# Three of four feed-forward blocks open with plain row blocks, their scratch is placed elsewhere, and the planner starts them with engines already busy

## The chip, the cores and the metric

The kernel runs on one core of a Trainium2 chip. The metric is the device time of one launch in microseconds (us); lower is better. An engine's name is as the profile has it: PE is the matmul engine, PEld its weight loads, DVE, ACT and POOL are the three elementwise engines, SP issues most of the DMAs.

## The reference, cut to what matters

A hybrid encoder of two layers works on 512 + 32 tokens of width 1024. Each layer has two SwiGLU feed-forward blocks at half step, so there are four feed-forward blocks in the program, and they alone are touched by the change. Between them lie a Mamba-2 mixer (first layer), an attention with shared keys and values (second layer), and a gated input at the end of each layer.

```python
def swiglu(h, w_gate, w_up, w_down):
    return (jax.nn.silu(h @ w_gate) * (h @ w_up)) @ w_down

x = x + 0.5 * swiglu(rms_norm(x, ffn_norm[i, 0]), ffn_w_gate[i, 0], ffn_w_up[i, 0], ffn_w_down[i, 0])
...
x = x + 0.5 * swiglu(rms_norm(x, ffn_norm[i, 1]), ffn_w_gate[i, 1], ffn_w_up[i, 1], ffn_w_down[i, 1])
```

## The kernel before, in words

All 544 tokens (T) stand side by side in the free dimension, in two halves of 272 (H); the 1024 model rows are 8 chunks of 128 (KC). Every float32 product is made of three matmuls: weight and input are each split into a high and a low part (`whi`/`wlo`, `xh`/`xl`, `hh`/`hl`), and high*high, high*low and low*high are added in PSUM. Splitting a 128x1024 weight is a copy (ACT or POOL) that gives `whi`, and a subtraction (mostly DVE) that gives `wlo`.

A feed-forward block (class `Sevens`, lines 532 to 893) has 22 row blocks of 128 hidden rows. A hidden row block needs a gate and an up product. There are two forms:

- the plain form (unit "p", called the old form in the change's title): for one row block and one of gate/up, 8 chunks x 3 matmuls x 2 halves = 48 matmuls of 128x272. The method `plain` (line 824) then multiplies both products by the norm's factor `r` out of PSUM into two scratch tiles `g` and `u`, applies silu, multiplies, and splits the result into `hh` and `hl` (`hidden`).
- the form by sevens (unit "s"): two row blocks at once by a Strassen-Winograd scheme, seven products in place of eight. Each of the seven steps (`STEPS`, line 530) is 4 chunks x 2 x 3 = 24 matmuls of 128x272. It needs sums of weight quarters (`s`, `a`; DVE or POOL), sums of input quarters (`xf`, class `Forms`, made once per feed-forward block by ACT and DVE), and four scratch tiles `c0` to `c3`, into which ACT copies intermediate products out of PSUM (`save`, line 775: steps 0, 1, 2 and 4 go to `c0`, `c3`, `c1`, `c2`).

`FIRST` (line 49) lists the row blocks of the opening group of each feed-forward block; a pair in parentheses goes by sevens. `GROUPS` lists the other groups, all pairs. After each group its part of the down product follows, interleaved with the next group's steps. The four PSUM banks have the roles A, B, D, X; plain blocks use (A, B) and (D, X) in turn.

The order of instructions on PE, DVE, ACT and POOL in a feed-forward block is set by a planner (class `Plan`, line 61) while the program is built: every piece of work is a generator that asks for slots of a resource ("get"), events ("wait") or engine time, and the planner repeatedly emits the request that can start earliest by its own cost table. `plan.busy` is the time until which it takes an engine as occupied when the block starts: zero for all, and 3.0 for PE in the first block (which has an opening by hand, `opening`, line 428). The planner also picks ACT or POOL for a copy and DVE or POOL for a sum by the load it has booked. `raw` is a resource of two buffers (`wraw`) through which all plain and down weights come from memory; weight quarters for the form by sevens have buffers of their own (`a11` to `a22`).

The norm of a block is worked out beside its first products: PE sums the squares with a matrix of minus ones (tile `nones`, right operand names `hh`/`hl`), ACT and DVE make `r` from the result. Blocks one, two and four do so; block three takes `r` ready from the norm before.

Of the kernel before, what the change touches and what calls it, by code (L numbers as in the profile page):

```python
# [4 lines left out]
F32 = mybir.dt.float32  # L5
# [5 lines left out]
P = 128  # L11
# [4 lines left out]
T = TP + TS  # L16
# [29 lines left out]

RGNORM, RSCAN, RCONV, RGATE, ROUT, RSTEP = 39, 4, 20, 45, 2, 41

FIRST = [0, 1, 2, 3], [0, 1, (2, 3)], [0, 1, (2, 3)], [0, 1, (2, 3)]
GROUPS = [(4, 5), (6, 7)], [(8, 9), (10, 11)], [(12, 13), (14, 15)], [(16, 17), (18, 19), (20, 21)]  # L50
AFTER, UNTIL = 3, 14

NH = 6
# [117 lines left out]
def s_cost(n, psum=False):  # L171
    return n / 1200.0 + (0.052 if psum else 0.094)


def v_cost(n):
    return n / 960.0 + 0.069


def _body(tc, io):
# [17 lines left out]
    V, S, G, TE = (Engine(n, e) for n, e in (("V", nc.vector), ("S", nc.scalar), ("G", nc.gpsimd), ("T", nc.tensor)))  # L197
# [4 lines left out]
    with ExitStack() as ctx:  # L202
        const = ctx.enter_context(tc.tile_pool(name="const", bufs=1))
        pool = ctx.enter_context(tc.tile_pool(name="pool", bufs=1))

        def halves(ap):
            return ap.rearrange("p (a b) -> p a b", a=2)
# [324 lines left out]
        class Sevens:  # L532
# [7 lines left out]
            def __init__(self, plan, i, norm, bank, tmp, ring, roles, after, first=(), opened=None, ahead=None, done=None):  # L540
                self.plan, self.i, self.bank, self.tmp, self.ring = plan, i, bank, tmp, ring
                self.groups, self.after, self.opened, self.norm, self.ahead, self.done = (FIRST[i],) + GROUPS, after, opened, norm, ahead, done
                self.roles, self.first = list(roles), first
# [279 lines left out]

            def plain(self, f, pg, pu, banks):
                yield "wait", "r"
                places = ("c2", "c3") if f % 2 else ("sq", "sq")
                for t in places:
                    yield "get", t
                g, u = (self.tmp.tile([P, T], F32, tag=t, name=t) if f % 2 else pool.tile([P, T], F32, tag=t, name=t, bufs=2) for t in places)
                rv = halves(self.norm.r[:, :])  # L830
                yield "W", v_cost(T), lambda: V.tensor_tensor(out=halves(g[:, :]), in0=pg[:, :, :H], in1=rv, op=ALU.mult)
                yield "put", f"b{banks[0]}"
                yield "S", s_cost(T), lambda: S.activation(g, g, AF.Silu), "silu"
                yield "W", v_cost(T), lambda: V.tensor_tensor(out=halves(u[:, :]), in0=pu[:, :, :H], in1=rv, op=ALU.mult)
                yield "put", f"b{banks[1]}"
                yield from self.hidden(f, g, u)
                for t in places:
                    yield "put", t
# [38 lines left out]
            def run(self):  # L877
                plan, (A, B, D, X) = self.plan, self.roles
                self.plain_banks = (A, B), (D, X)
                if self.opened:  # L880
                    plan.busy["T"] = 3.0
                    plan.add(-1, self.first_block((A, B)))
                plan.add(0, self.scale(X))
                plan.add(20, self.dense())
                plan.add(10, self.weights())
                plan.add(9, self.fetch_plain())
                for name in ("a11", "a21", "a22", "a12"):
                    plan.add(9, self.fetch_quarter(name))
                plan.add(5, self.sums())
                ordered.update("TVSG")  # L890
                plan.run()
                ordered.clear()
                return [self.loaded[len(self.units) - 1]] if self.ahead is not None else ()

        def sevens(i, norm, after, bank, tmp, ring, roles, **kw):
            slots = {f"b{k}": 1 for k in range(4)}
            slots.update({f"c{k}": 1 for k in range(4)})
            slots.update({"raw": 2, "w": Sevens.NW, "a11": 1, "a21": 1, "a22": 1, "a12": 1, "s3": 1, "s2": 1, "gu0": 1, "gu1": 1, "sq": 2, "h": NH})
            return Sevens(Plan(slots, "ff"), i, norm, bank, tmp, ring, roles, after, **kw).run()

        def ple_inputs(i, tmp):
# [525 lines left out]
        def attention(norm, after, ready, ahead, kT, vtok):  # L1427
            with ExitStack() as keep, \
# [33 lines left out]
                with tc.tile_pool(name="at", bufs=1, reuse_waits="tile") as tmp:  # L1462
# [66 lines left out]
                    class Stream:  # L1529
# [66 lines left out]
                        def passed(self, kb, b, t):  # L1596

                            yield "wait", ("sum", self.name, kb + 1, b)
                            yield "get", "run"
                            old = self.run[kb + 1, b]  # L1600
                            run = self.run[kb, b] = tmp.tile([P, 512], F32, tag="run", name="run", bufs=NRUN)
                            yield either(plan, v_cost(512), 1.225, lambda e: e.tensor_tensor(out=run, in0=old, in1=t, op=ALU.add))
                            yield "set", ("sum", self.name, kb, b)
                            yield "spawn", self.release(kb, b)
                            yield "get", "s"
                            sh, sl = parts_tile()
                            yield from halve(run, sh, sl)
                            self.sums[kb, b] = sh, sl
                            yield "set", (self.name, kb, b)
# [310 lines left out]
        V.tensor_copy(identb, ident)  # L1920
        nm0 = Norm("m0")
        ready = sevens(0, n00, nm0.ops, bank, tmp, ring_of(tmp, "h", NH), (2, 3, 1, 0), opened=opened, ahead=io["win"][40])
        st.close()
        sp.close()
# [7 lines left out]
        def second_half(i, norm, name, first, done=lambda: None):  # L1932

            sh, hidden = space("fh")
            st, tmp = space("ff")

            def open_np():
                done()
                later["st"], later["pool"] = space("np", "right")

            after = Norm(name, ring=lambda: ring_of(later["pool"], "n", KC)())
            sevens(i, norm, after.ops, bank, tmp, ring_of(hidden, "h", NH), roles(), first=first, done=open_np)
            st.close()
            return sh, after
# [14 lines left out]
        nm1 = Norm("m1")  # L1959
        st, tmp = space("ff")  # L1960
        ready = sevens(2, n10, nm1.ops, bank, tmp, ring_of(tmp, "h", NH), roles(), first=first, ahead=io["wq"][0])
        st.close()
        sp.close()
# [9 lines left out]
        acc = pool.tile([P, T], F32, tag="acc", name="acc")  # L1973
# [122 lines left out]
```

## Time and profile before

| | |
|---|---|
| three timed runs | 2366.95, 2370.83, 2382.75 us; median 2370.83 |
| the profiled execution | 2376.65 us |
| its span, first to last instruction | 2374.9 us |
| busy PE / PEld | 2315.3 us (97%) / 2220.8 us (94%) |
| busy DVE / ACT / POOL | 1753.1 us (74%) / 1057.4 us (45%) / 608.1 us (26%) |
| HBM traffic | 204.83 MB read, 5.58 MB written |

The four feed-forward blocks fill about 0 to 415 us, 844 to 1250 us, 1313 to 1690 us and 1905 to 2310 us of the span. Busy PE is an upper figure, since matmuls overlap in the pipe; the steady distance between matmuls is what counts. A wait is shown as the idle time in front of an instruction, with the instruction that ended it. The granted clock is that of PE: 1.00 is 2.4 GHz, 0.50 is 1.2 GHz, and a figure between is a mean over a stretch that has both.

### The profile page before, as it was taken

Reading aid. Unit: us, or ns where it says so; the run is one execution under the profiler, and the core shown is the slowest. Engines: PE = TensorE matmul, PEld = TensorE weight load, DVE = VectorE, ACT = ScalarE, POOL = GpSimd, SP = SyncE. Lnnn points to the kernel's source line nnn. Section 1 sums busy time; section 2 is a strip of 40 time slices with the busy share of each in tenths; the row PEclk is TensorE's granted clock in tenths of the full one; section 3 lists DMA queues with packets and bytes.
Section 4 is the critical chain, followed back from the end, with each engine's and each line's share of the span. In section 5 each row is a group of like instructions: output and inputs, shape, how many; then the busy total and the mean of one; then the engine's idle time right before and its main releaser. Section 6 shows DMA issues by size and latency. Waiting matters only on the chain.

```text
span 2374.9 us, 42488 instructions
## 1 busy us (share of the span) xinstructions
PE 2315.3 (97%) x17687; PEld 2220.8 (94%) x17694; DVE 1753.1 (74%) x2268; ACT 1057.4 (45%) x1542; POOL 608.1 (26%) x582
## 2 busy tenths in 40 slices
PE   8999999989999999999999999999999999999997
PEld 8999999979999999999999899999964799999997
DVE  7777786777767677777857877777678687777757
ACT  5333334476646343333354433333578553333344
POOL 3222222244323132122211222221334132221214
PEclk9999999989999999999999999999999999999999
DMA  4233322333333232333233332332211132333232
GB/s 156 82 97 104 93 72 89 101 94 104 88 100 96 80 107 72 106 91 103 65 102 98 116 98 83 97 103 68 88 41 32 36 107 81 103 94 102 64 103 74
DMA packets 113617, 213.15 MB, mean 90 GB/s; under 512 B 12529, under 2 KB 34545, under 8 KB 113425
## 3 DMA queue, kind: packets, MB, share of 16 engines
q1 hardware_dynamic: 110640, 204.92, 28.3%
q10 hardware_dynamic: 2784, 5.52, 0.7%
q8 instruction: 139, 2.28, 0.4%
q14 instruction: 54, 0.43, 0.1%
HBM read 204.83 MB, written 5.58 MB: 89 GB/s over the span
## 4 chain that ended last, share of the span: by engine, by line
PE 90%; DVE 5%; ACT 2%; issue 1%; DMA 1%; POOL 0%; SPq 0%; DVEq 0%; ACTq 0%; POOLq 0%
PE mm L191 79%; PE z L191 5%; PE aux L191 4%; DVE wlo L191 1%; PE f L191 1%; PE o L191 1%; DVE xl L191 1%; ACT whi L191 1%; DVE x L191 1%; DVE sl L191 0%; DMA wraw<-in_wpg 0%; DVE hl L191 0%; DVE fu L191 0%; DMA wraw<-in_wgu 0%; ACT zt L191 0%
## 5 line engine op out<-in xcount | busy, mean ns | idle before, releaser
L191 PE MATMUL mm<-xh,whi 128*128 128x272 f32 x1976 | 498.2, 295 | 2.0 <-ACT xh L191 1.4
L191 PE MATMUL mm<-xl,whi 128*128 128x272 f32 x1976 | 493.0, 293 | 3.0 <-DVE xl L191 3.0
L191 PE MATMUL mm<-xh,wlo 128*128 128x272 f32 x1976 | 490.5, 291 | 3.4 <-DVE wlo L191 3.4
L191 PE MATMUL mm<-xfh,whi 128*128 128x272 f32 x1248 | 363.2, 291 | 14.2 <-ACT c L191 11.6
L191 PE MATMUL mm<-xfl,whi 128*128 128x272 f32 x1248 | 362.5, 290 | 0.0
L191 PE MATMUL mm<-xfh,wlo 128*128 128x272 f32 x1248 | 362.2, 290 | 0.0
L191 PEld LDWEIGHTS mm<-xh,whi 128*128 128x128 f32 x1976 | 345.7, 192 | 11.2 <-issue 7.8
L191 PEld LDWEIGHTS mm<-xl,whi 128*128 128x128 f32 x1976 | 345.8, 192 | 4.0 <-DVE xl L191 3.9
L191 PEld LDWEIGHTS mm<-xh,wlo 128*128 128x128 f32 x1976 | 345.3, 192 | 4.3 <-DVE wlo L191 4.3
L191 ACT ACTIVATE whi<-wraw 128x1024 fp32r<-128x1024 f32 (+3 forms) x205 | 175.4, 857 | 379.9 <-PE mm L191 257.5
L191 DVE TENSOR_TENSOR wlo<-wraw,whi 128x1024 fp32r<-128x1024 f32 (+3 forms) x247 | 249.1, 1009 | 65.5 <-ACT whi L191 55.0
L191 PE MATMUL mm<-hh,whi 128*128 128x272 f32 x1408 | 291.3, 288 | 0.0
L191 ACT ACTIVATE whi<-a 128x1024 fp32r<-128x1024 f32 x133 | 141.2, 1061 | 336.8 <-PE mm L191 212.2
L191 PE MATMUL mm<-hh,wlo 128*128 128x272 f32 x1408 | 290.9, 288 | 0.0
L191 PE MATMUL mm<-hl,whi 128*128 128x272 f32 x1408 | 290.9, 288 | 0.0
L191 DVE TENSOR_TENSOR wlo<-a,whi 128x1024 fp32r<-128x1024 f32 x154 | 191.5, 1243 | 100.4 <-ACT whi L191 63.6
L191 PEld LDWEIGHTS mm<-xfh,whi 128*128 128x128 f32 x1248 | 237.5, 190 | 15.6 <-ACT c L191 11.0
L191 PEld LDWEIGHTS mm<-xfh,wlo 128*128 128x128 f32 x1248 | 237.7, 190 | 0.0
L191 PEld LDWEIGHTS mm<-xfl,whi 128*128 128x128 f32 x1248 | 237.7, 190 | 0.0
L191 PEld LDWEIGHTS mm<-hl,whi 128*128 128x128 f32 x1408 | 221.2, 188 | 0.0
L191 PEld LDWEIGHTS mm<-hh,whi 128*128 128x128 f32 x1408 | 221.0, 188 | 0.0
L191 PEld LDWEIGHTS mm<-hh,wlo 128*128 128x128 f32 x1408 | 220.7, 188 | 0.2 <-DVE wlo L191 0.2
(290 smaller groups left out, 4290.9 us busy)
## 6 DMA issues: line engine op xcount, KB each, us to landing
a<-in_wgu SPq DMA_DIRECT2D x156, 512.0 KB, 3.9
wraw<-in_wd SPq DMA_DIRECT2D x128, 256.0 KB, 2.7
wraw<-in_win SPq DMA_DIRECT2D x41, 512.0 KB, 3.6
wraw<-in_wd SPq DMA_DIRECT2D x32, 384.0 KB, 3.2
wraw<-in_wgu SPq DMA_DIRECT2D x18, 512.0 KB, 3.7
ab<-acs_d SPq DMA_DIRECT2D x16, 512.0 KB, 4.7
wraw<-in_wout SPq DMA_DIRECT2D x16, 512.0 KB, 3.6
wraw<-in_wpg SPq DMA_DIRECT2D x16, 512.0 KB, 3.6
```

Source lines behind the costliest of these rows:

```text
L191: ins = getattr(self.engine, op)(*args, **kw)
```

## The change

Four edits in three places. `FIRST` now opens every feed-forward block with four plain row blocks, as block one did before. In `plain`, odd row blocks (the second and the fourth) keep `g` in the tile `acc` and `u` in `c2`, where they had `c2` and `c3`; `acc`, which holds the sum of squares until the norm is made, becomes a resource of the planner. And the planner of blocks two to four starts with DVE, ACT and POOL booked until 6.0, 4.5 and 4.0 us.

```diff
-FIRST = [0, 1, 2, 3], [0, 1, (2, 3)], [0, 1, (2, 3)], [0, 1, (2, 3)]
+FIRST = [0, 1, 2, 3], [0, 1, 2, 3], [0, 1, 2, 3], [0, 1, 2, 3]
...
-                places = ("c2", "c3") if f % 2 else ("sq", "sq")
+                places = ("acc", "c2") if f % 2 else ("sq", "sq")
                 for t in places:
                     yield "get", t
-                g, u = (self.tmp.tile([P, T], F32, tag=t, name=t) if f % 2 else pool.tile([P, T], F32, tag=t, name=t, bufs=2) for t in places)
+                g, u = (self.tmp.tile([P, T], F32, tag=t, name=t) if t == "c2" else pool.tile([P, T], F32, tag=t, name=t, bufs=1 + (t == "sq")) for t in places)
...
+                plan.busy.update({"T": 3.0} if self.opened else {"V": 6.0, "S": 4.5, "G": 4.0})
                 if self.opened:
-                    plan.busy["T"] = 3.0
...
-            slots.update({"raw": 2, "w": Sevens.NW, "a11": 1, "a21": 1, "a22": 1, "a12": 1, "s3": 1, "s2": 1, "gu0": 1, "gu1": 1, "sq": 2, "h": NH})
+            slots.update({"raw": 2, "w": Sevens.NW, "a11": 1, "a21": 1, "a22": 1, "a12": 1, "s3": 1, "s2": 1, "gu0": 1, "gu1": 1, "sq": 2, "acc": 1, "h": NH})
```

On PE, in block two, this is the end of row block 1's up product (`mm_9703`) and what follows it, in the kernel before:

```order
L191 MATMUL mm_9703<-xl7_9435,whi_9584 128x272 x2
L191 MATMUL mm_9703<-xh7_9434,wlo_9585 128x272 x2
L191 MATMUL mm_9770<-xh0_9201,whi_9634 128x272
L191 MATMUL mm_9770<-xl0_9202,whi_9634 128x272
L191 MATMUL mm_9770<-xh0_9201,wlo_9635 128x272
```

The single matmuls into `mm_9770` are the first of the seven steps. At the same place of the changed kernel (row block 1's up product is `mm_9702` there):

```order
L191 MATMUL mm_9702<-xl7_9435,whi_9596 128x272 x2
L191 MATMUL mm_9702<-xh7_9434,wlo_9597 128x272 x2
L191 MATMUL mm_9768<-xh0_9201,whi_9629 128x272 x2
L191 MATMUL mm_9768<-xl0_9202,whi_9629 128x272 x2
L191 MATMUL mm_9768<-xh0_9201,wlo_9630 128x272 x2
```

The gate product of row block 2 stands there, and three more plain products (row block 2's up, row block 3's two) before the first step by sevens.

On ACT, in block two, this is the stretch of the first steps in the kernel before; `c0`, `c1`, `c3` and `c2` out of `mm` are the copies of step results, `c2<-c2` the silu of row block 1, and `hh<-c3` the high part of its hidden rows:

```order
L191 ACTIVATE c0_9811<-mm_9770 128x544
L191 ACTIVATE xfh3_9472<-gu1_9780 128x1088
L191 ACTIVATE whi_9838<-a21_9484 128x1024
L191 ACTIVATE c2_9777<-c2_9777 128x544
L191 ACTIVATE whi_9871<-a22_9486 128x1024
L191 ACTIVATE c1_9909<-mm_9770 128x544
L191 ACTIVATE whi_9943<-a11_9733 128x1024
L191 ACTIVATE hh_9948<-c3_9778 128x544
L191 ACTIVATE c3_9956<-mm_9840 128x544
L191 ACTIVATE c2_9957<-mm_9770 128x544
```

The same stretch of the changed kernel, with the silu of row block 3 in `acc`:

```order
L191 ACTIVATE acc_10027<-acc_10027 128x544
L191 ACTIVATE whi_10052<-wraw_9825 128x512
L191 ACTIVATE c0_10062<-mm_10020 128x544
L191 ACTIVATE whi_10088<-s2_10054 128x1024
L191 ACTIVATE whi_10124<-wraw_9876 128x512
L191 ACTIVATE c3_10133<-mm_10090 128x544
L191 ACTIVATE whi_10158<-a21_9484 128x1024
L191 ACTIVATE c1_10198<-mm_10020 128x544
L191 ACTIVATE whi_10222<-a22_9486 128x1024
L191 ACTIVATE c2_10263<-mm_10020 128x544
```

The input forms (`xfh`) all stand ahead of this stretch now, the copy to `c3` comes second instead of third, with no hidden tile in `c3` ahead of it, and weights of the down product (`wraw`, 128x512) stand between the copies.

On DVE, this is the start of block two in the kernel before, from the last addition to the sum of squares to the low part of that sum (`hl<-acc`), for which PE's sum for the norm waits:

```order
L191 TENSOR_TENSOR acc_9217<-acc_9217,sq_9440 128x544
L191 TENSOR_TENSOR gu1_9510<-gu0_9477 128x544
L191 TENSOR_TENSOR wlo_9506<-wraw_9478,whi_9505 128x1024
L191 SCALAR_TENSOR_TENSOR gu1_9510<-gu1_9510,gu0_9477 128x272
L191 TENSOR_TENSOR wlo_9508<-wraw_9480,whi_9507 128x1024
L191 SCALAR_TENSOR_TENSOR gu1_9510<-gu1_9510,gu0_9477 128x272
L191 TENSOR_TENSOR xfl0_9473<-gu1_9510,xfh0_9469 128x1088
L191 TENSOR_TENSOR hl_9575<-acc_9217,hh_9574 128x544
```

And in the changed kernel:

```order
L191 TENSOR_TENSOR acc_9217<-acc_9217,sq_9440 128x544
L191 TENSOR_TENSOR wlo_9504<-wraw_9478,whi_9503 128x1024
L191 TENSOR_TENSOR gu1_9542<-gu0_9477 128x544
L191 TENSOR_TENSOR wlo_9506<-wraw_9480,whi_9505 128x1024
L191 SCALAR_TENSOR_TENSOR gu1_9542<-gu1_9542,gu0_9477 128x272 x2
L191 TENSOR_TENSOR hl_9571<-acc_9217,hh_9570 128x544
L191 TENSOR_TENSOR xfl0_9473<-gu1_9542,xfh0_9469 128x1088
```

The first weight's low part moved ahead of the input form's first sum, and `hl<-acc` ahead of `xfl0`. On ACT, `hh<-acc` moved ahead of the second input form in the same stretch. In block one no instruction changes its place; only the names of the scratch tiles do.

## Rows read from the trace of the kernel before

**Rows 1.** The page's head and busy time of each engine, whole span.

```profile
span 2374.9 us, 42488 instructions
PE 2315.3 (97%) x17687; PEld 2220.8 (94%) x17694; DVE 1753.1 (74%) x2268; ACT 1057.4 (45%) x1542; POOL 608.1 (26%) x582
```

**Rows 2.** Waits of PE, whole span: releaser, total us, times, longest.

```profile
PE mm L191 <- ACT c L191: 11.6, 6, 4.2
...
PE mm L191 <- DVE c L191: 2.6, 1, 2.6
...
PE mm L191 <- DVE hl L191: 2.2, 2, 1.1
...
PE mm L191 <- ACT hh L191: 1.2, 2, 0.6
```

**Rows 3.** Timeline of PE: start, us, instruction, idle before it and its releaser.

```profile
851.73 0.52 PE L191 MATMUL mm<-xh,wlo 128*128 128x272 f32 x2 [1.87 <-DVE wlo L191]
...
894.71 0.60 PE L191 MATMUL mm<-xfh,whi 128*128 128x272 f32 x1 [4.18 <-ACT c L191]
...
1345.99 0.37 PE L191 MATMUL mm<-xfh,whi 128*128 128x272 f32 x1 [2.57 <-DVE c L191]
...
1965.59 0.60 PE L191 MATMUL mm<-xfh,whi 128*128 128x272 f32 x1 [4.18 <-ACT c L191]
```

**Rows 4.** Windows: us, PE, PEld, DVE, ACT, POOL busy (count); clock, DMA share, GB/s.

```profile
858.60:880.00 21.40, 21.40 (x161) 21.40 (x160) 17.61 (x24) 11.86 (x14) 5.34 (x3) 0.92 0.12 38
894.70:905.00 10.30, 10.29 (x65) 10.30 (x66) 5.56 (x7) 2.45 (x4) 2.39 (x2) 0.77 0.13 49
1340.00:1358.80 18.80, 14.42 (x101) 13.83 (x99) 17.04 (x17) 6.94 (x10) 6.10 (x5) 0.91 0.25 85
1927.50:1951.00 23.50, 22.41 (x164) 22.18 (x165) 19.67 (x26) 13.27 (x15) 6.67 (x4) 0.93 0.11 34
1965.60:1976.00 10.40, 10.40 (x63) 10.40 (x64) 5.28 (x7) 2.18 (x3) 2.39 (x2) 0.73 0.15 49
30.00:450.00 420.00, 420.00 (x3344) 419.67 (x3343) 317.10 (x380) 158.10 (x208) 95.58 (x98) 1.00 0.30 90
```

**Rows 5.** Timeline of DVE and ACT, block two, around the longest wait.

```profile
889.21 1.88 DVE L191 TENSOR_TENSOR hl<-sq,hh 128x544 fp32r<-128x544 f32 x1
891.01 1.21 DVE L191 TENSOR_TENSOR s<-a,a 128x1024 f32<-128x1024 f32 x1
892.15 1.21 DVE L191 TENSOR_TENSOR wlo<-a,whi 128x1024 fp32r<-128x1024 f32 x1
893.28 0.71 DVE L191 TENSOR_TENSOR hl<-c,hh 128x544 fp32r<-128x544 f32 x1
...
894.03 1.14 ACT L191 ACTIVATE c<-mm 128x544 f32<-128x544 f32 x2 [1.98 <-DVE hl L191]
```

**Rows 6.** Timeline of DVE and ACT, block two, around the sum for the norm.

```profile
849.82 0.71 DVE L191 TENSOR_TENSOR gu<-gu 128x544 f32<-128x544 f32 x1
850.46 1.21 DVE L191 TENSOR_TENSOR wlo<-wraw,whi 128x1024 fp32r<-128x1024 f32 x1
851.59 0.43 DVE L191 SCALAR_TENSOR_TENSOR gu<-gu,gu 128x272 f32<-128x272 f32 x1
...
855.90 0.64 ACT L191 ACTIVATE hh<-acc 128x544 fp32r<-128x544 f32 x1
...
856.60 1.57 DVE L191 TENSOR_TENSOR hl<-acc,hh 128x544 fp32r<-128x544 f32 x1
```

**Rows 7.** Timeline of SP, POOL and DVE: fetch and splitting of a plain weight.

```profile
851.70 0.34 SPq L266 DMA_DIRECT2D wraw<-in_wgu  x1
...
856.42 1.17 POOL L191 TENSOR_SCALAR whi<-wraw 128x1024 fp32r<-128x1024 f32 x1 [7.09 <-DMA wraw<-in_wgu]
...
1323.47 3.42 DVE L191 TENSOR_TENSOR wlo<-wraw,whi 128x1024 fp32r<-128x1024 f32 x1
```

## The prediction

> **What bounds the kernel now.** I read the page's head first: PE is busy 97% of the span and its weight loads 94%, DVE comes next with 74% [rows 1]. So time is matmuls one behind the other, plus the few stretches in which PE stands still or runs at half clock. The second view is the list of PE's waits [rows 2]: its longest entry is "PE waits for ACT c", six times, 11.6 us. The third is PE's timeline, which puts these waits in place [rows 3]: they lie where the form by sevens starts in feed-forward blocks two, three and four. The fourth is the windows [rows 4]: the same stretches show a granted clock of 0.73 to 0.91. The reader is to see there too that block one, which opens with four plain row blocks already, has none of this: from 30 to 450 us PE is busy 420.00 of 420.00 us at clock 1.00.
>
> Why PE waits in block two: the copies of step results into scratch (ACT, c<-mm) stand behind row block 1's hidden tile in c3. At 893.28 DVE makes its low part, hl<-c; until then c3 is not free, and only then, at 894.03, ACT copies the step results, after 1.98 us of idling for that DVE instruction [rows 5]. PE goes on at 894.71, after 4.18 us [rows 3]. DVE was late because it had the input forms, the norm, the weight sums and the plain blocks' tail to do at once. Block four's wait has the same length, 4.18 us. In block three the wait is split, 2.57 us for a DVE drain and the rest for ACT.
>
> **What the change adds.** A pair by sevens is 7 x 24 = 168 matmuls, two plain row blocks are 4 x 48 = 192. Three blocks get 24 more each: 72. The price of one is 420.00 us / 3344 = 125.6 ns [rows 4]. All lie on the path, since PE is the bound: 72 x 0.1256 = **+9.0 us**. Weights cost no more traffic (a pair is four loads of 512 KB either way), and DVE, ACT and POOL have less to do, as plain blocks need no weight sums.
>
> The Trainium skill ("TensorE: Matmul & The Clock Gate", "Wait — 56ns, not 53.3ns?") gives back-to-back matmuls at full clock as columns / 2.4 GHz plus 2.5 ns; for 272 columns that is an estimate of 115.8 ns, and the sum would be 8.3 us. The trace has 125.6 ns for this very shape, with a weight load for each matmul, so the measurement decides.
>
> **What it takes away at the start of the sevens.** ACT's six waits are 11.6 us and DVE's one is 2.6 us [rows 2]: 14.2 us, the long ones of which are in [rows 3]. Behind them, PE runs some us at 1.2 GHz. What this costs is window times (1 - clock) [rows 4]: 10.30 x 0.23 = 2.4 in block two, 18.80 x 0.09 = 1.7 in block three, 10.40 x 0.27 = 2.8 in block four, together 6.9. As a cross-check by count, 65 matmuls took 10.3 us where 65 x 0.1256 = 8.2 would do, so 2.1 for the first. Term: 14.2 + 6.9 = **-21.1 us**, if no wait takes the place.
>
> What stands in the place: two more plain row blocks give PE 192 x 0.1256 = 24 us of work before the first step by sevens, during which DVE can finish the input forms and the norm. The next thing that could be late is the first pair's chain (drain of row block 3, the sums s3 and s2, the copies c0 and c3). Block one has the same row blocks, the same order of steps and the same scratch pressure, and no wait at all after 30 us [rows 4]; there DVE is busy 317.10 of 420 us. That is the nearest row, and I take zero. The bounds are zero and the full 21.1 (below).
>
> **What the planner's new start takes away.** With engines booked at the start, hl<-acc moves ahead of xfl0, and hh<-acc ahead of the second input form. Before, PE waited for hh and hl in blocks two and four, 1.2 + 2.2 us [rows 2]. The low part of the first weight ended at 850.46 + 1.21 = 851.67; on the new list gu (0.71), wlo (1.21), two of 0.43 and hl (0.71, the hl of [rows 5]) follow, which ends near 855.2 [rows 6]. PE reaches the sum for the norm at about 856, just ahead of where ACT makes hh today (855.90). So both waits go: **-3.4 us**. The wait for the first wlo (1.87 us in block two [rows 3]) I leave standing: it still comes behind the sum of squares, and the gu that is moved behind it saves 0.7 us at most. The half-clock stretch behind these waits costs 21.40 x 0.08 = 1.7 and 23.50 x 0.07 = 1.6 us [rows 4]. It may stay because of that first wait; I do not count it. Bounds of this term: nothing, and 3.4 + 3.3 + 1.9 = 8.6.
>
> **Edits at nothing.** The scratch in acc and c2 frees c3 for the second step's copy, which belongs to the term above; in block one no instruction changes its place and no wait is there to lose, so zero. The weight feed is the cover that could go: eight plain weights in a row through two buffers. A fetch issued at 851.70 is split from 856.42 on, 4.7 us, then 1.17 and 1.2 to 3.4 us for the halves [rows 7], so 7.1 to 9.3 us per buffer, or 3.6 to 4.7 us per weight with two. PE takes 48 x 0.1256 = 6.0 us for one. It would bind only if a buffer's round took over 12.1 us.
>
> **Sum.** +9.0 - 21.1 - 3.4 = -15.5 us against the profiled 2376.65 us (span 2374.9 us and 1.75 us around it), so 2361.2. That execution is 5.8 us over the median of the runs, 2370.83; against the median the forecast is **2355.3 us**.
>
> **Rivals.** (a) *Half of the start's waits stay.* DVE is busy 17.04 of 18.80 us around block three's start [rows 4], and it now has four more weight subtractions before it. If half of 21.1 comes back as waits in the first pair, the sum is -15.5 + 10.5 = -5.0: 2365.8 us. Against it: block one.
> (b) *The wait moves along and the matmuls are paid for nothing.* Place: the first steps of pair (4, 5) in blocks two to four, where ACT's copy into c2 waits for row block 3's hidden tile, as it waited for c3. Blocks two to four start with DVE still draining the stage before; block one doesn't. Price: all 24.5 us stay and 9.0 is added: 2379.8 us, slower. It decides sign from the point where under 9.0 of the 24.5 us is saved. Against it: the longest wait is 4.18 us [rows 3], and DVE now gets 24 us more ahead of the place. The Trainium skill ("Perfetto Trace Analysis", "Identifying Performance Opportunities") says to improve the most-contended engine, for PE to be judged by weight-load share; with 94% here the change lengthens just that engine's work, which by itself speaks for this rival. The page's next step, to find what blocks that engine in its gaps, is what the other terms rest on.
> (c) *The clock stays up as well.* Without the waits for hh and hl the stretches behind them run at 2.4 GHz and the first wlo comes in time: 5.2 us more, 2350.1 us.
>
> **How the numbers follow.** Forecast 0.62, (a) 0.20, (b) 0.08, (c) 0.10. The runs before reach 3.9 us below and 11.9 us above their median. The low end is (c) less that 3.9, with a little beyond: 2345. The high end is (a) plus most of the upward scatter, 2374, which leaves out most of (b). Under or over 1% (23.7 us, about what a measurement of this kernel tells from no change) is 2347.1 or 2394.5: the first is reached by (c), or by the forecast on a fast day, 0.10; the second only by (b) with more on top, 0.03; the rest 0.87.
>
> **What would show it.** Right: 72 more matmuls in all, with 96 fewer of each kind with xfh or xfl (three pairs of four steps of 8); the waits on ACT c and DVE c fall from 14.2 us to under 2; the window of 15 us after each start of the sevens has clock 1.00; waits on hh and hl are gone; POOL's and DVE's busy times fall. Wrong: an "ACT c" or "DVE wlo" wait of some us at the first steps of pair (4, 5); a "DMA wraw" or "DVE wlo" wait inside row blocks 2 and 3; a half-clock stretch in that place.

## The result and the profile after

The changed kernel takes 2349.36 us (median of four runs, 2348.45 to 2351.84), the kernel before 2373.22 us in the same comparison. The ratio is 0.9903, with a 95% interval of 0.9874 to 0.9931: 23 us faster, or 16 to 30. The forecast was 2355.3 us, 15.5 us faster, with a range of 2345 to 2374.

The page's head and the busy times, the lines that answer to [rows 1]:

```profile
span 2346.7 us, 42561 instructions
PE 2307.8 (98%) x17759; PEld 2216.6 (94%) x17766; DVE 1714.5 (73%) x2236; ACT 1048.6 (45%) x1530; POOL 592.2 (25%) x575
```

PE issues 72 instructions more (17759 against 17687), as worked out, and DVE 32 fewer. The longest waits of PE, to be held against [rows 2]:

```profile
PE aux L191 <- DVE xd L191: 6.0, 3, 4.2
PE z L191 <- DVE sl L191: 3.2, 4, 1.3
PE aux L191 <- POOL ab L191: 2.7, 2, 1.5
```

The first and third belong to the mixer, the second to the attention. No wait on ACT c, DVE c, ACT hh or DVE hl is left in the whole list. In the windows at the same places as [rows 4] (columns as there; the starts have moved with the time; the second is block two from the third step by sevens on), the granted clock is 1.00 throughout:

```profile
848.00:870.00 22.00, 22.00 (x178) 22.00 (x177) 19.64 (x25) 11.11 (x15) 6.17 (x5) 1.00 0.32 98
892.60:903.00 10.40, 10.40 (x86) 10.40 (x85) 6.83 (x9) 3.90 (x5) 3.04 (x4) 1.00 0.26 66
1351.00:1361.00 10.00, 10.00 (x82) 10.00 (x81) 6.67 (x8) 3.68 (x5) 2.75 (x3) 1.00 0.26 67
1952.20:1963.00 10.80, 10.80 (x88) 10.80 (x87) 7.29 (x9) 3.90 (x5) 2.98 (x3) 1.00 0.28 81
```

The reader is to see PE busy for every microsecond, and 86 matmuls in 10.40 us at the third step by sevens where 65 took 10.30 us before. What became of the place in [rows 5]: ACT and DVE around the first steps of pair (4, 5) in block two, which begin at 886.54 us.

```profile
888.77 0.72 DVE L191 TENSOR_TENSOR c<-mm,r 128x544 f32<-128x544 f32 x1
889.59 0.72 DVE L191 TENSOR_TENSOR c<-c,acc 128x544 f32<-128x544 f32 x1
890.24 1.22 DVE L191 TENSOR_TENSOR s<-s,a 128x1024 f32<-128x1024 f32 x1
892.84 0.72 DVE L191 TENSOR_TENSOR c<-mm,c 128x544 f32<-128x544 f32 x1 [1.39 <-PE mm L191]
...
890.20 0.61 ACT L191 ACTIVATE c<-mm 128x544 f32<-128x544 f32 x1
...
896.27 0.61 ACT L191 ACTIVATE c<-mm 128x544 f32<-128x544 f32 x1
```

The roles have changed: DVE waits 1.39 us for PE's product, and ACT's copies of step results follow other work without idling for DVE. The opening of block two, which answers to [rows 6]:

```profile
842.23 1.22 DVE L191 TENSOR_TENSOR wlo<-wraw,whi 128x1024 fp32r<-128x1024 f32 x1
...
843.50 0.52 PE L191 MATMUL mm<-xh,wlo 128*128 128x272 f32 x2 [0.71 <-DVE wlo L191]
...
842.40 0.66 ACT L191 ACTIVATE hh<-acc 128x544 fp32r<-128x544 f32 x1 [0.22 <-DVE acc L191]
...
845.96 0.72 DVE L191 TENSOR_TENSOR hl<-acc,hh 128x544 fp32r<-128x544 f32 x1
...
847.62 0.41 PE L191 MATMUL mm<-hh,nones 128*128 128x272 f32 x2
847.87 0.42 PE L191 MATMUL mm<-hl,nones 128*128 128x272 f32 x2
```

The sum for the norm (the two lines into `nones`) finds both operands ready and starts without a wait: hl ends at 846.68, four microseconds after hh begins. The first wlo wait is 0.71 us instead of 1.87.

**By stage.** The timeline of PE gives each block's time between fixed instructions: block two from the mixer's last output matmul to the first matmul of the gated input (mm<-nh), block three from the last transposition of the values to the attention's first product, block four from the attention's last product to the first mm<-nh. Idle is PE's idle time inside.

| us | before, profiled | changed, profiled |
|---|---|---|
| block two | 393.7 (idle 8.5) | 384.1 (idle 0.7) |
| block three | 375.0 (idle 4.4) | 371.4 (idle 0.0) |
| block four | 393.7 (idle 7.7) | 384.1 (idle 0.7) |
| mixer, between blocks one and two | 452.2 | 445.5 |
| attention | 227.7 | 229.0 |

The three blocks give 9.6 + 3.5 + 9.6 = 22.7 us. The 6.7 us in the mixer, whose instructions do not change, are a matter of chance, as the experiments show (below); so nearly all of the medians' 23.9 us is in the blocks. The two profiled executions are further apart, 28.2 us, by the mixer's share.

### The profile page after: what moved, and what is told of

Its sections match the earlier page's. It is cut to its first block, busy times and chain, and to the rows that moved or that the text cites. A ratio compares the mean times of both kernels' runs of the same rounds, so it can differ in the third digit from the quotient of the medians.

```text
span 2346.7 us, 42561 instructions
## 1 busy us (share of the span) xinstructions
PE 2307.8 (98%) x17759; PEld 2216.6 (94%) x17766; DVE 1714.5 (73%) x2236; ACT 1048.6 (45%) x1530; POOL 592.2 (25%) x575
## 4 chain that ended last, share of the span: by engine, by line
PE 92%; DVE 4%; ACT 2%; DMA 1%; issue 1%; POOL 0%; SPq 0%; DVEq 0%; ACTq 0%; POOLq 0%
PE mm L191 81%; PE z L191 5%; PE aux L191 4%; PE f L191 1%; PE o L191 1%; DVE wlo L191 1%; DVE xl L191 1%; ACT whi L191 1%; DVE x L191 1%; DMA x<-in_x 0%; DMA wraw<-in_wpg 0%; DVE fu L191 0%; DVE sl L191 0%; ACT zt L191 0%; POOL ab L191 0%
## 5 line engine op out<-in xcount | busy, mean ns | idle before, releaser
L191 PE MATMUL mm<-xh,whi 128*128 128x272 f32 x2096 | 514.3, 293 | 1.1 <-ACT whi L191 0.5
L191 PE MATMUL mm<-xl,whi 128*128 128x272 f32 x2096 | 509.9, 291 | 2.5 <-DVE xl L191 2.5
L191 PE MATMUL mm<-xh,wlo 128*128 128x272 f32 x2096 | 508.4, 291 | 2.1 <-DVE wlo L191 2.1
L191 PEld LDWEIGHTS mm<-xh,wlo 128*128 128x128 f32 x2096 | 360.3, 190 | 2.9 <-DVE wlo L191 2.9
L191 PE MATMUL mm<-xfh,whi 128*128 128x272 f32 x1152 | 332.0, 288 | 0.0
L191 PE MATMUL mm<-xfl,whi 128*128 128x272 f32 x1152 | 331.9, 288 | 0.0
L191 PE MATMUL mm<-xfh,wlo 128*128 128x272 f32 x1152 | 331.7, 288 | 0.0
L191 PEld LDWEIGHTS mm<-xfh,wlo 128*128 128x128 f32 x1152 | 216.8, 188 | 0.0
L191 PEld LDWEIGHTS mm<-xfl,whi 128*128 128x128 f32 x1152 | 216.8, 188 | 0.0
L191 PEld LDWEIGHTS mm<-xfh,whi 128*128 128x128 f32 x1152 | 216.7, 188 | 0.0
```

The source lines that it names most:

```text
L191: ins = getattr(self.engine, op)(*args, **kw)
```

## The experiments

All medians stand beside runs of the kernel before on the same chip: 2375.73 us (28 runs) for the first four kernels, 2371.59 us (11 runs) for the next four, 2374.32 us (7 runs) for the last two. "By stage" means the three blocks measured as in the table, 1162.4 us together in the first profile of the kernel before. Theory A says that DVE had no time at the start of the sevens, and that two more plain row blocks give it that time. Theory B says that the hidden tile in c3 was the cause, theory C that the planner's order was.

**One edit alone: FIRST.**

```diff
-FIRST = [0, 1, 2, 3], [0, 1, (2, 3)], [0, 1, (2, 3)], [0, 1, (2, 3)]
+FIRST = [0, 1, 2, 3], [0, 1, 2, 3], [0, 1, 2, 3], [0, 1, 2, 3]
```

> Only FIRST is changed: four plain row blocks, scratch and planner start as before. Theory A (the start of the sevens waited because DVE had no time): waits on ACT c and DVE c go from 14.2 us to under 2, 72 matmuls cost 9.0, and the waits on hh and hl (3.4 us) stay: 10 to 13 us faster than before. Theory B (the hidden tile in c3 is what held the copies): the wait moves to row block 3, which still uses c2 and c3, 8 us or more of ACT c waits remain, and the kernel is 3 us faster to 9 us slower.

2357.63 us, ratio 0.9917 (0.9892 to 0.9941), 20 us faster where 10 to 13 were expected. The mechanism is A's: no ACT c or DVE c wait is left. These are all of PE's waits from 840 to 1000 us, and from 1890 to 2000 us:

```profile
PE mm L191 <- DVE wlo L191: 1.9, 1, 1.9
...
PE mm L191 <- ACT hh L191: 0.9, 1, 0.9
PE mm L191 <- DVE hl L191: 0.8, 1, 0.8
PE mm L191 <- DVE wlo L191: 0.5, 1, 0.5
PE mm L191 <- DVE x L191: 0.3, 1, 0.3
PE mm L191 <- ACT whi L191: 0.3, 1, 0.3
```

By stage the blocks take 386.8, 371.1 and 388.6 us, 15.9 us less together. In block two the sum for the norm no longer waits, but not because DVE and ACT are sooner:

```profile
851.13 0.64 ACT L191 ACTIVATE hh<-acc 128x544 fp32r<-128x544 f32 x1
851.83 0.72 DVE L191 TENSOR_TENSOR hl<-acc,hh 128x544 fp32r<-128x544 f32 x1
852.59 0.42 PE L191 MATMUL mm<-hh,nones 128*128 128x272 f32 x2
```

ACT makes hh 4.17 us after the first wlo matmul (which starts at 846.96), as in the kernel before (855.90 after 851.73). It is PE that comes later: it runs at 1.2 GHz for 3.4 us right behind the wlo wait and reaches the sum 5.63 us after that matmul, where it took 4.87 before. So those waits hid behind matmuls that ran slower, and the opening's half clock stays, 3.4 us in block two and 3.4 us in block four; what is gone of it is at the sevens.

**One edit alone: the scratch.**

```diff
-                places = ("c2", "c3") if f % 2 else ("sq", "sq")
+                places = ("acc", "c2") if f % 2 else ("sq", "sq")
...
```

(and the two lines that go with it in the change above)

> Only the scratch of odd row blocks is moved to acc and c2; blocks two to four still open with a pair by sevens. Theory A: DVE is as late as before, the longest waits change their releaser at most; 0 to 5 us faster. Theory B: the two 4.18 us waits and the half clock behind them go, 12 to 20 us faster, without the 9.0 us of matmuls.

2361.86 us, ratio 0.9941 (0.9920 to 0.9962). The time lies where B put it, but the trace bears B out only in part: PE's idle time in the three blocks is 9.1, 4.2 and 5.1 us where it was 8.5, 4.4 and 7.7. PE's timeline in block two, at the start of the sevens:

```profile
876.60 0.55 PE L191 MATMUL mm<-xfh,whi 128*128 128x272 f32 x1 [3.97 <-DVE acc L191]
...
885.07 0.39 PE L191 MATMUL mm<-xfh,whi 128*128 128x272 f32 x1 [0.71 <-ACT c L191]
...
893.00 0.37 PE L191 MATMUL mm<-xh,whi 128*128 128x272 f32 x1 [1.68 <-ACT c L191]
```

The wait of 4.18 us for the hidden tile shrinks to 1.68 us, in block four too: 2.5 us of it hung on c3. In block two one of 3.97 us for DVE's drain of row block 1 stands ahead of it; the kernel before has one like it there in its second profile (below), so it is not shown to come from the edit. So the tile in c3 made the wait longer, and most of the idle time, which DVE's lateness makes, stayed. What is faster here is mainly the clock: at 1.2 GHz PE ran 3.4 us in block two instead of 10.2, 0 instead of 3.4 in block three, and 3.4 instead of 10.2 in block four, 17.1 us less. What that is worth shows in the distance of matmuls in the kernel before:

```profile
859.06 0.66 PE L191 MATMUL mm<-xl,whi 128*128 128x272 f32 x2
859.51 0.66 PE L191 MATMUL mm<-xh,wlo 128*128 128x272 f32 x2
```

Two matmuls take 0.45 us there, 226 ns each where 125.6 is usual. Part of the time at 1.2 GHz falls on waits and costs nothing; by the starts of PE's matmuls, 91 of them run at that distance in the three blocks of the kernel before, which is 9.4 us lost, and 29 here, 2.9 us. With the 2.1 us of idle time that makes 8.6 us, and by stage the blocks are 8.5 us faster (392.4, 372.9, 388.6). The rest of the 14 us lies outside the blocks. A's 0 to 5 us was too narrow: it left the clock out, and the share of c3.

**One edit alone: the planner's start.**

```diff
+                plan.busy.update({"T": 3.0} if self.opened else {"V": 6.0, "S": 4.5, "G": 4.0})
```

> Only the planner's start is changed. Theory A: the 3.4 us of waits on hh and hl go, with part of the first wlo wait and perhaps the half clock behind them (3.3 us); the start of the sevens keeps its 14 us of waits: 3 to 8 us faster. Theory C (the planner's order was what mattered at the sevens too): the waits on ACT c fall under 5 us as well, 15 us faster or more.

2362.95 us, ratio 0.9952 (0.9929 to 0.9975), 11 us where A had 3 to 8. The waits on hh and hl are gone and the first wlo wait is 0.71 us, but the sevens still wait:

```profile
873.14 0.57 PE L191 MATMUL mm<-xfh,whi 128*128 128x272 f32 x1 [2.75 <-DVE c L191]
...
879.12 0.39 PE L191 MATMUL mm<-xfl,whi 128*128 128x272 f32 x1 [1.44 <-DVE xfl L191]
...
886.18 0.37 PE L191 MATMUL mm<-xfh,whi 128*128 128x272 f32 x1 [1.62 <-ACT c L191]
```

Three waits of 5.8 us in block two where there were two of 4.9. ACT c alone does fall under 5 us (to 4.0), as C had it, but DVE c, DVE wlo, DVE xfl and ACT xfh take its place, and the waits at the sevens of the three blocks are 17.2 us where they were 14.2: C falls. The blocks are 6.9 us faster (391.3, 373.0, 391.2), within A's range; PE ran 6.8, 0 and 3.4 us at 1.2 GHz.

**Scratch and planner without FIRST** (the two diffs above together).

> FIRST is left as before, scratch and planner start are changed. Theory A: gains of the planner's start alone, 3 to 10 us faster than before, so 12 us or more slower than the full change. Theory B with C: all waits go without the 72 matmuls, about 29 us faster than before and 9 us faster than the full change.

2367.6 us, ratio 0.9965 (0.9944 to 0.9986): 8 us faster, as A had it, and far from B with C. At the start of the sevens in block two PE waits 2.75 us on DVE acc and 1.43 us on DVE xfl. That this comes out above either edit alone (2361.86, 2362.95) does not show in the blocks (391.3, 373.0, 389.9 us, 8.2 us faster): it goes with the clock of its runs, 0.985 on average where the ten runs with the scratch alone had 0.988. That is about 14 us more at 1.2 GHz in a run, or some 6 us, and the one profile has only 3.4 us of it in the blocks.

**The full change again.**

> The full change once more, to size it against many runs of before. Theory A with rival (c): 20.7 us from the feed-forward blocks, 19 to 25 us faster. In the profile the mixer's time (between blocks one and two, untouched by the change) is the open part: if its half-clock time is a lottery, it lies anywhere between 445 and 452 us in this run; if the change shortens it, it is about 445.5 again.

2348.16 us (6 runs), ratio 0.9903 (0.9882 to 0.9924). The blocks repeat to 0.1 us, 384.1, 371.4 and 384.2. The mixer took 454.9 us in this profile, against 445.5 in the first, and above the 452 that were expected at most. The window of the mixer in the two profiles of the changed kernel:

```profile
391.10:836.60 445.50, 436.86 (x3498) 412.67 (x3496) 332.16 (x564) 250.04 (x403) 139.77 (x174) 0.97 0.33 95
```

and in the second:

```profile
391.10:846.00 454.90, 445.73 (x3497) 420.48 (x3496) 332.13 (x564) 250.44 (x402) 139.43 (x174) 0.95 0.33 93
```

The same instructions on every engine, but the granted clock is 0.97 in one and 0.95 in the other.

**The change without the planner's start, and without the scratch.**

> The full change without the planner's start (all engines from zero in blocks two to four). Theory A: as with FIRST alone, the sevens start without a wait, while the sum for the norm keeps waits of about 2 us and the first wlo 1.9 us with half clock behind them in blocks two and four: 4 to 8 us slower than the full change. Rival: the planner's start matters at the sevens too, then ACT c or DVE c waits come back.

> The full change without the moved scratch (odd row blocks in c2 and c3). Theory A: DVE has time, row block 3's hidden tile is out of c3 before the second step's copy, and the kernel is within 2 us of the full change. Theory B (the tile in c3 is a wait of its own): a wait of 1 to 4 us on ACT c at the second or third step in blocks two to four, and 4 to 15 us slower than the full change.

Without the planner's start (FIRST and scratch): 2356.46 us, 8.3 us slower than the full change in the same comparison, just above A's range. The sevens start without a wait, and the opening has its waits back:

```profile
845.85 0.52 PE L191 MATMUL mm<-xh,wlo 128*128 128x272 f32 x2 [1.88 <-DVE wlo L191]
...
850.73 0.52 PE L191 MATMUL mm<-hh,nones 128*128 128x272 f32 x2 [0.59 <-ACT hh L191]
```

By stage it is 386.7 against 384.1 in block two and 388.6 against 384.2 in block four, together 7.0 us, of which idle time is 4.1 and half clock, in block four alone, 1.5. Without the moved scratch (FIRST and planner): 2348.91 us, 0.8 us from the full change. In block two its only wait up to 1000 us is the first wlo, 0.7 us. By stage it is 0.4 us, and FIRST alone and FIRST with the scratch differ by 0.1 us. So the scratch edit is worth nothing once DVE has time.

**What a matmul costs on the path.**

```diff
+                            if e == 0 and 0 < g < 4 and not self.opened:
+                                product(to, self.loaded[j], parts, only=e, close=True)
                             yield "T", 0.753, lambda: product(to, self.loaded[j], parts, only=e)
```

> The full change, with the first six matmuls of each down product of groups 1 to 3 in blocks two to four issued twice (the second issue starts the sum anew, so the values stay): 3 blocks x 3 groups x 8 x 6 = 432 matmuls of 128x272 more, no other engine's instruction moved. If a matmul costs 125.6 ns on the path, 54.3 us slower than the full change; if part of them hides in waits, less; by 115.8 ns each it is 50.0 us.

2404.43 us, 56.3 us over the full change, or 130 ns for each of the 432. By stage, which chance in the mixer does not touch, the blocks are 402.3, 389.5 and 402.4 us, 18.2 + 18.1 + 18.2 = 54.5 us more: 126 ns each. No matmul hid in a wait. By the 115.8 ns that the prediction estimated from the Trainium skill ("TensorE: Matmul & The Clock Gate", "Wait — 56ns, not 53.3ns?") it would have been 50.0 us; the trace, with 126 ns, does not agree.

**The kernel before again.**

> The kernel before, profiled once more. If the mixer's time is a lottery of the clock, it is anywhere between 445 and 452 us here; if the change shortened the mixer, it is near 452 again. The feed-forward blocks repeat 393.7, 375.0 and 393.7 us within 1 us, with waits on ACT c and DVE c of 14.2 us.

2382.61 us, one run. Blocks three and four repeat (374.9 and 393.7 us); block two took 397.1, as its sevens waited once more than in the first profile. So the waits on ACT c and DVE c are 18.1 us, not 14.2 as expected:

```profile
884.83 0.42 PE L191 MATMUL mm<-xfh,whi 128*128 128x272 f32 x1 [3.98 <-DVE c L191]
...
893.28 0.39 PE L191 MATMUL mm<-xfh,whi 128*128 128x272 f32 x1 [0.71 <-ACT c L191]
...
900.68 0.60 PE L191 MATMUL mm<-xfh,whi 128*128 128x272 f32 x1 [4.14 <-ACT c L191]
```

The mixer took 455.1 us, again above the expected 452. Over all twelve profiles, of kernels that do not differ there, it took 445.5 to 455.1 us, and those of the full change hold nearly both ends (445.5, 454.9): chance, not the change. The clock of whole runs says the same. It is 0.9835 on average over 46 runs of the kernel before and 0.9883 over ten of the full change, which is an estimate of 78 and 55 us at 1.2 GHz in a run; the 23 us between them are the 23.9 us that the three blocks lost, so the rest of the program had as much on average with the change as without.

**DVE's load taken away.** The kernel before, with pairs by sevens in the opening; the low part of the input forms is set to zero by ACT and so left out of the result:

```diff
-                yield "V", v_cost(4 * H), lambda: V.tensor_tensor(out=l, in0=s, in1=h.bitcast(F32), op=ALU.subtract)
+                yield "S", s_cost(4 * H), lambda: S.activation(l, s, AF.Copy, scale=0.0)
```

> The kernel before (pairs by sevens in the opening), but the low part of the input forms is set to zero by ACT instead of being subtracted on DVE: 16 instructions of 1.3 us leave DVE, 4 in each feed-forward block, and the low parts of the forms are left out of the result. Theory A (DVE had no time at the start of the sevens): waits on ACT c and DVE c fall from 14.2 us to under 7, 8 to 18 us faster than before with the half clock behind them. Theory B (the scratch conflict as such): the waits stay over 10 us and the time is within 4 us of before.

2351.75 us, ratio 0.9895 (0.9862 to 0.9928), 25 us faster where 8 to 18 were expected. The first two rows of its wait list:

```profile
PE aux L191 <- DVE xd L191: 6.2, 3, 4.3
PE mm L191 <- ACT c L191: 5.3, 5, 2.1
```

DVE c is gone and ACT c is 5.3 us; together they were 14.2 us before. No wait at the sevens is over 2.2 us, and half clock in the three blocks falls from 23.9 to 3.4 us. In block two this is the first step by sevens, the low part of row block 1's hidden tile and the copy that waits for it:

```profile
865.50 0.29 PE L191 MATMUL mm<-xh,whi 128*128 128x272 f32 x1
...
880.64 0.71 DVE L191 TENSOR_TENSOR hl<-c,hh 128x544 fp32r<-128x544 f32 x1
...
881.45 0.63 ACT L191 ACTIVATE c<-mm 128x544 f32<-128x544 f32 x1 [2.21 <-DVE hl L191]
```

ACT still idles for that DVE instruction, but it comes 15.1 us after the first step, where it came 18.9 us after it in the kernel before (893.28 after 874.41). Neither the scratch nor FIRST is touched here, which fits A: DVE's time accounts for most of the waits. Two things moved along and were not separated from it. The planner sets its order by its costs, so it drew up another order and gave DVE five instructions back (x2257, where 2268 less 16 is 2252): DVE is busy 12.7 us less, not 20.8. And the matmuls with the low part read zeros here; whether that touches the clock no run shows, but the idle time, which fell from 20.5 to 9.9 us, does not hang on it.

The blocks are 386.0, 372.8 and 385.7 us, 17.9 us faster than before, inside the expected range, and 4.8 us slower than with the change: 9 us of matmuls less, but 8.5 us of waits more and what comes behind them. A way to take that work off DVE with the low parts kept was not tried.

## Why the prediction was right, and where it was off

- *What bounds the kernel.* Right. PE is the bound, the waits lay at the start of the sevens, and DVE's lateness was their cause, with c3 as a part of it; moving 16 instructions off DVE did as much in the blocks as FIRST alone (17.9 and 15.9 us). What is open there is the planner's order, which moved along.
- *The added matmuls, +9.0 us.* Right: 126 ns each by stage, 54.5 us for 432. The 125.6 ns taken from the trace is what a matmul costs here.
- *The start of the sevens, -21.1 us.* Right in mechanism and nearly in size. With the +9.0 it should leave -12.1; FIRST alone gave -15.9 in the blocks. Of the difference, 1.7 us are the waits for hh and hl in block two, which were booked with the planner's start. About 2.5 us more are matmuls right behind a wait, which start further apart than the others: behind the 4.18 us of [rows 3] the next one starts 0.39 us on, at 895.10, and the ones after it every 0.23 us. No term had them. The nearest row, block one without waits, was the right guide: no wait took the place.
- *The planner's start, -3.4 us.* This is the step that was mis-sized. The waits on hh and hl did go, but the first wlo wait, which was left standing with 0.7 us at most to gain, fell by 1.16 us, from 1.87 to 0.71, in block two, and the half clock behind the opening (3.3 us), which was not counted, went as well. On top of FIRST and scratch the edit is worth 7.0 us in blocks two and four and 8.3 us by medians.
- *Scratch at nothing.* Right within 0.8 us beside the other edits; alone it is worth 8.5 us in the blocks.
- *The weight feed.* Right: no DMA wait appears in row blocks 2 and 3.
- *Rivals.* (c), with a chance of 0.10, is what happened. That its 2350.1 us is within 0.8 us of the measured 2349.36 is luck: it takes 20.7 us off a median of 2370.83, the blocks gave 22.7 us, and the median beside the result was 2373.22. Nor did the first wlo come in time; it kept 0.71 us. (a) and (b) did not happen; row block 3's hidden tile was out of the way in time, even in c3. The doubt that kept the clock out of the forecast was not idle: with FIRST alone, a stretch at half clock stood behind the first wlo wait of 1.86 us by itself, while with FIRST and scratch block two had that wait (1.88 us) and no such stretch.

The sum as measured, from the two profiles: idle time in the three blocks 20.5 - 1.4 = 19.1 us, 91 matmuls at half clock 9.4 us, matmuls +9.0: -19.5 us, against 22.7 by stage. The other 3.2 us are matmuls that start further apart, most of them right behind a wait.

## What to carry to other kernels

When the bound engine waits for a late helper, look for work of its own that needs nothing from the helper: here 72 more matmuls, 9 us, together with the planner's start, removed 19.1 us of waits and 9.4 us of lost clock. Give the half-clock stretch behind a wait a term and a chance of its own: here all of them in the blocks went with the waits, but the same wait had such a stretch behind it in one run and none in another. And compare a stage between fixed instructions: it repeated to 0.1 us in the changed kernel where whole runs scattered by 11 us; in the kernel before, one of the three blocks differed by 3.4 us between its two profiles.

## What was not expected of the hardware

In the mixer, with the same instructions and nearly the same waits (8.5 and 8.6 us of idle PE), PE ran at 1.2 GHz for 41.0 us in the first profile of the kernel before and 23.9 us in that of the changed kernel, 44.4 us in each one's second profile (9.2 us of idle PE in both). That moves the mixer by up to 9.6 us from one run to the next, as much as the cost of all the added matmuls. And the sum of the waits did not tell the time at half clock: with the scratch alone moved, idle time in the three blocks fell by only 2 us, but the time at 1.2 GHz from 23.9 to 6.8 us. In block three the two waits stayed (2.57 and 1.63 us), and the 3.4 us at 1.2 GHz behind the first were gone. What decides it is not shown.
